# Splitting four weight blocks by one cast and one subtraction in a decoder layer with two feed-forward halves

## The chip, the cores and the metric

One core of a Trainium2 chip runs the whole layer as one program. The metric is the device time of one execution in microseconds (us), of which the median of three runs is quoted. The engines are named as in the profile: PE (matmul) with PEld (its weight loads), DVE (vector engine), ACT (scalar engine), POOL, and SP, whose queue issues all the transfers spoken of here.

## The reference

The reference is one decoder layer on 256 tokens of 2048 values in float32: a first SwiGLU half step, a mixing part (differential attention and a convolution group between one input and one output projection), cross-attention into 256 memory tokens, and a second SwiGLU half step. The change touches the two half steps (called FFN1 and FFN2 here):

```python
def swiglu(h, w_gate, w_up, w_down):
    return (jax.nn.silu(h @ w_gate) * (h @ w_up)) @ w_down

x = x + 0.5 * swiglu(rms_norm(x, ffn1_norm_g[l]), ffn1_w_gate[l], ffn1_w_up[l], ffn1_w_down[l])
...
x = x + 0.5 * swiglu(rms_norm(x, ffn2_norm_g[l]), ffn2_w_gate[l], ffn2_w_up[l], ffn2_w_down[l])
```

The weights are 2048x5632 (gate, up) and 5632x2048 (down), in float32.

## The kernel before

**Split numbers.** A float32 product is made of three matmuls on a rounded format (fp32r): every operand is split into a high part (a cast) and a low part (the operand minus the high part), and high x high, high x low and low x high are added in PSUM. The activations are split once. Every weight block must be split when it arrives: `split` (line 145) issues a cast on ACT (line 146) that writes a tile `wh`, and a subtraction on DVE (line 147) that reads the landed weights `raw` and `wh` and writes `wl`. A block is 128 rows by 512 columns.

**Parts.** `quad` (line 200) does the FFN products. It works through parts; a part is two 128-row blocks of each of two weight matrices, so four blocks, in one tile `raw` of 128x4x512. Two transfers on SP's queue bring them (lines 228 and 229; one 512 KB each). There are three `raw` tiles (`RAWS` = 3, line 27). For an ordinary part the four blocks are split by two casts and two subtractions of 1024 columns (lines 230 and 234), and PE does 24 matmuls of 512 columns (lines 278 to 282). A part with sums, called a seven here, multiplies a 2x2 arrangement of blocks by seven products instead of eight: three of the blocks are split as they come (two by one cast and one subtraction of 1024 columns, line 230, the third by one of 512, line 232), DVE makes sums of the blocks in place in `raw` (lines 242, 244 and 245: 1024, 512 and 512 columns), and the four results are split by two more casts and subtractions of 1024 columns (lines 247 and 248). PE then does 21 matmuls (`passes`, line 195, called in lines 260 to 266). The split tiles come in pairs `wh`, `wl` of two blocks each from the pool `wf`, which holds seven of each (`SPLITS`, lines 27, 141 and 411); an ordinary part takes two pairs, a seven takes four.

**Chunks and passes.** `ffn` (line 410) goes through 11 chunks of 512 gate and up columns, in groups of 4, 4 and 3. A chunk is one call of `quad` with 8 parts, of which parts 1, 3 and 5 are sevens (`S_IN`, line 29); only the very first chunk of FFN1 has none. After a group two passes of the down product follow, each with 8 parts and three sevens, or, for the group of 3, with 6 parts and two sevens (`S_DOWN`, `ORDER_DOWN`, lines 33 and 34). In both half steps together there are 264 parts, of which 95 are sevens, 168 ordinary, and one, the first of all, is split block by block (lines 217 to 226).

**What ends a chunk.** After the last seven `middle` (line 429) calls `combine` (line 287): ACT copies the PSUM tile `p1`, DVE forms `us` from the PSUM tile `q6` (line 292), then `vw` (line 294) and `ys` (line 432). At the end of the chunk `evac` (line 436) adds these to the PSUM sums into new tiles `full` (line 441), takes the silu into a new tile `s` on ACT (line 444) and multiplies on DVE (line 446). `turn` (line 449), due seven steps later, or two after the last chunk of a group, transposes the result on PE (line 452). The transposed blocks go to PSUM tiles of the same two slots (`tpp`) that `p1` and `q6` occupied, so the second group of transposes can start only when `us` has been computed.

**Order.** The program states the order of the work; the tool that builds the program places instructions of each engine in an order of its own by its estimate of when they can run, and each engine then runs its queue in that fixed order. `later` and `step` (lines 71 to 83) say after how many parts deferred work is stated.

**Between the half steps.** Pools opened after FFN1 (lines 644 to 647: `memp`, the weight pools of the middle part, and `mix` in line 688) take the memory that FFN1's pools had, and FFN2's pools take theirs. `proj` (line 150), which does all the products in between, splits two blocks at a time by one cast and one subtraction.

Of the kernel before, what the change touches and what calls it, by code (L numbers as in the profile page):

```python
# [7 lines left out]
F32 = mybir.dt.float32  # L8
F32R = mybir.dt.float32r
# [3 lines left out]
ALU = mybir.AluOpType  # L13
# [3 lines left out]
P = 128  # L17
# [6 lines left out]
START_S = 6  # L24
LOADS_X = (1, 2, 2, 3, 3, 4, 4, 4)
WARM = 8
RAWS, SPLITS, H_BUFS = 3, 7, 2

S_IN = (1, 3, 5)
ORDER_0 = tuple(range(8))  # L30
# [23 lines left out]
def hybrid_layer(ctx, tc, x, head, xT, mem, memT, pos, convw, bvec, w):  # L54
    nc = tc.nc
    V, S, T, G = nc.vector, nc.scalar, nc.tensor, nc.gpsimd
# [9 lines left out]
    ph = {}  # L66
# [60 lines left out]
    def behind(ins):  # L127

        order = ExitStack()
        for i in ins:  # L130
            order.enter_context(tc.issue_after(i.ins))
        return order
# [3 lines left out]
            fn()  # L136

    def weight_tiles():
        return ph["raw"].tile([P, 2, 512], F32, tag="raw", name="raw"), *split_tiles()

    def split_tiles():
        return (ph["wh"].tile([P, 2, 512], F32R, tag="wh", name="wh"),
                ph["wl"].tile([P, 2, 512], F32R, tag="wl", name="wl"))

    def split(raw, wh, wl):
        last[:] = [S.copy(out=wh, in_=raw),  # L146
                   V.tensor_tensor(out=wl, in0=raw, in1=wh.bitcast(F32), op=ALU.subtract)]  # L147
# [44 lines left out]
    def rows_pair(wsrc, row):  # L192
        return wsrc[row * P:(row + 2) * P, :].rearrange("(c p) n -> p c n", p=P)
# [6 lines left out]
    def quad(parts, srcs, middle, evac, first=False):  # L200

        acc = [[accp.tile([P, 512], F32, tag=f"acc{tb}{j}", name=f"acc{tb}{j}") for j in range(2)]
               for tb in range(2)]
        begun = set()
        seven = [i for i, p in enumerate(parts) if p()[4]]  # L210
        q = None
        for n, part in enumerate(parts):
            h, l, i0, row, sums = part()

            raw = ph["raw"].tile([P, 4, 512], F32, tag="raw", name="raw")
            wa, wb = split_tiles(), split_tiles()
            if first and n == 0:

                for b in range(2):
                    for j in range(2):  # L220
                        pos = (0, 1, 3, 2)[2 * b + j]
                        nc.sync.dma_start(out=raw[:, pos, :], in_=srcs[j][(row + b) * P:(row + b + 1) * P, :])
                        t = wa if pos < 2 else wb
                        with behind(first_x):
                            split(raw[:, pos, :], t[0][:, pos % 2, :], t[1][:, pos % 2, :])
                    first_hooks[b]()
            else:
                nc.sync.dma_start(out=raw[:, 0:4:3, :], in_=rows_pair(srcs[0], row))
                nc.sync.dma_start(out=raw[:, 1:3, :], in_=rows_pair(srcs[1], row))
                split(raw[:, 0:2, :], *wa)  # L230
                if sums:
                    split(raw[:, 3, :], wb[0][:, 1, :], wb[1][:, 1, :])
                else:
                    split(raw[:, 2:4, :], *wb)
            ev0, ev1, od1, od0 = [tuple(t[:, c, :] for t in w) for w in (wa, wb) for c in range(2)]

            def at(b, tb):
                return [t[:, i0 + b, tb * P:(tb + 1) * P] for t in (h, l)]

            if sums:  # L240

                V.tensor_tensor(out=raw[:, 1:3, :], in0=raw[:, 1:3, :], in1=raw[:, 2:4, :], op=ALU.add)  # L242

                V.tensor_tensor(out=raw[:, 3, :], in0=raw[:, 3, :], in1=raw[:, 1, :], op=ALU.add)
                V.tensor_tensor(out=raw[:, 0, :], in0=raw[:, 0, :], in1=raw[:, 3, :], op=ALU.add)
                wc, wd = split_tiles(), split_tiles()
                split(raw[:, 1:3, :], *wc)
                split(raw[:, 0:4:3, :], *wd)
                t3, t1, t4, t2 = [tuple(t[:, c, :] for t in w) for w in (wc, wd) for c in range(2)]
                sh, sl = sums  # L250

                def s(c):
                    return [t[:, c, :] for t in (sh, sl)]

                if q is None:
                    q = {"p1": tpp.tile([P, 512], F32, tag="tp", name="p1"),
                         "q6": tpp.tile([P, 512], F32, tag="tp", name="q6"),
                         "q57": ph["q"].tile([P, 2, 512], F32, tag="q57", name="q57")}
                st, sp = n == seven[0], n == seven[-1]
                passes(acc[0][0], *at(0, 0), ev0, "00" not in begun, False)  # L260
                passes(acc[0][1], *s(3), ev1, "01" not in begun, False)
                passes(q["p1"], *at(1, 0), od0, st, sp)
                passes(q["q57"][:, 1, :], *s(2), t3, st, sp)
                passes(q["q57"][:, 0, :], *s(0), t1, st, sp)
                passes(acc[1][0], *at(0, 1), t4, "10" not in begun, False)
                passes(q["q6"], *s(1), t2, st, sp)
                begun |= {"00", "01", "10"}
                if sp:
                    middle(q)
            else:  # L270
                ending = n == len(parts) - 1
                wt = [[ev0, ev1], [od0, od1]]
                for tb in range(2):
                    for js in ([[0], [1]] if ending else [[0, 1]]):
                        for b in range(2):
                            hs, ls = at(b, tb)
                            for j in js:
                                T.matmul(acc[tb][j], hs, wt[b][j][0], start=f"{tb}{j}" not in begun, stop=False)  # L278
                                begun.add(f"{tb}{j}")
                                T.matmul(acc[tb][j], hs, wt[b][j][1], start=False, stop=False)  # L280
                            for j in js:
                                T.matmul(acc[tb][j], ls, wt[b][j][0], start=False, stop=(ending and b == 1))  # L282
                    if ending:
                        evac(tb, acc[tb])
            step()
# [122 lines left out]


    def ffn(norm, wg, wu, wd, groups, done):  # L410
        with tc.tile_pool(name="wf", bufs=SPLITS, reuse_waits="tile") as wf, \
                tc.tile_pool(name="ffn", bufs=2, reuse_waits="tile") as fp, \
                tc.tile_pool(name="ht", bufs=max(groups), reuse_waits="tile") as hp, \
                tc.tile_pool(name="wfr", bufs=RAWS, reuse_waits="tile") as wfr, \
                tc.tile_pool(name="qp", bufs=1, space=PSUM) as qp:
            ph.update(h=hp, raw=wfr, wh=wf, wl=wf, f=fp, q=qp, sraw="sraw", xsf="xsf")
            c0 = 0
            for gi, ng in enumerate(groups):
                hts, hsums, hold = {}, {}, {}
                s_down = S_DOWN[ng]  # L420
                for c in range(c0, c0 + ng):
# [5 lines left out]
                    rest = {}  # L427
# [8 lines left out]
                    def evac(tb, acc, c=c, rest=rest, end=(c == c0 + ng - 1), pairs=(c - c0 < s_down)):  # L436
                        acc = list(acc)
                        for j in range(2):
                            if rest:
                                t = fp.tile([P, 512], F32, tag="full", name="full")  # L440
                                V.tensor_tensor(out=t, in0=acc[j], in1=rest[tb, j][0], op=rest[tb, j][1])
                                acc[j] = t
                        s = fp.tile([P, 512], F32, tag="s", name="s")
                        S.activation(out=s, in_=acc[0], func=AF.Silu, scale=norm.rs(tb))
                        h = fp.tile([P, 512], F32, tag="h", name="h", bufs=H_BUFS)
                        V.scalar_tensor_tensor(out=h, in0=acc[1], scalar=norm.rs(tb), in1=s,
# [125 lines left out]
        V.tensor_scalar(out=xqcol, in0=col(C_XQ), scalar1=P ** -0.5, scalar2=None, op0=ALU.mult)  # L572

    def constants_b():
        bv = ph["f"].tile([P, 384], F32, name="bv", bufs=1)
        nc.sync.dma_start(out=bv, in_=bvec.broadcast_to([P, 384]))
        lm = stat.tile([P, 2, 64], F32, tag="cs", name="lm", bufs=1)
        b4 = bv[:, :256].rearrange("p (a b d) -> p a b d", a=2, b=2)
# [45 lines left out]
        for qk in range(2):  # L624
            g = bv[:, 256 + 64 * qk:256 + 64 * qk + 16]
            for tb in range(2):
                for hf in range(2):
# [3 lines left out]
                                    op=ALU.mult)  # L631
                    V.scalar_tensor_tensor(out=ropeB[:, tb, qk, hf * 8:(hf + 1) * 8], in0=sn[:, tb, :],
                                           scalar=(1.0 if hf else -1.0), in1=go, op0=ALU.mult, op1=ALU.mult)

    later(10, lambda: behind_last(constants_a))
    later(11, lambda: behind_last(constants_b))

    n2 = Norm(G_MIX, "mix")
# [3 lines left out]

    mids = ctx.enter_context(ExitStack())
    memp = mids.enter_context(tc.tile_pool(name="memp", bufs=1, reuse_waits="tile"))
    for kind, bufs in (("wh", 5), ("raw", 4), ("wl", 5)):
        ph[kind] = mids.enter_context(tc.tile_pool(name="m" + kind, bufs=bufs, reuse_waits="tile"))
    atp = mids.enter_context(tc.tile_pool(name="atp", bufs=2, space=PSUM))
# [25 lines left out]
    for n in range(4):  # L673
        later(6 + 6 * n, lambda n=n: mem_group(n))

    kmT = memp.tile([P, 4, 256], F32, name="kmT")
    vm = [memp.tile([P, 512], F32, name=f"vm{tb}") for tb in range(2)]

    def mstats():
        return [(mgrp[k // 4][0], mgrp[k // 4][1], k % 4, k) for k in range(KD)]  # L680
# [7 lines left out]
    with tc.tile_pool(name="mix", bufs=1, reuse_waits="tile") as mp:  # L688
        uT = [mp.tile([P, 4, 30 + 256], F32, name=f"uT{c}") for c in range(2)]
        y = mp.tile([P, 8, 256], F32, name="y")  # L690
        vt = [[mp.tile([P, 512], F32, name=f"v{tb}{c}") for c in range(2)] for tb in range(2)]
        for c in range(2):
            G.memset(uT[c][:, :, 0:30], 0.0)

# [212 lines left out]
        for ct in range(8):  # L907
# [4 lines left out]
            for j in range(1, TAPS):  # L912
                V.scalar_tensor_tensor(out=yc, in0=u[:, j:j + 256], scalar=cw[:, j * 8 + ct:j * 8 + ct + 1],  # L913
                                       in1=yc, op0=ALU.mult, op1=ALU.add)
# [7 lines left out]
        for a in range(2):  # L922
            V.tensor_tensor(out=y[:, 4 * a:4 * a + 4, :], in0=y[:, 4 * a:4 * a + 4, :],
                            in1=pm.broadcast_to([P, 4, 256]), op=ALU.subtract)
# [136 lines left out]
    out = w["out"]  # L1061
# [45 lines left out]
```

## Time and profile before

| what | value |
|---|---|
| median of three runs | 1887.45 us (1886.5 to 1888.75) |
| the profiled execution's own time | 1892.69 us |
| its span in the profile | 1890.9 us |
| busy: PE, PEld, DVE, ACT | 1857.8, 1526.2, 1682.3, 1091.6 us |
| granted TensorE clock, mean | 0.996 of full speed |
| read from HBM | 361.09 MB, 192 GB/s over the span |

The span is the stretch from the first to the last instruction of the profiled execution; its own time is 1.8 us longer and is 5.24 us above the median of the runs shown. Busy time of PE counts the modelled length of matmuls that overlap, so how close PE is to its pace is read from the distance between the starts of matmuls and from its gaps.

### The profile page before, as it was taken

Reading aid. Unit: us, or ns where it says so; the run is one execution under the profiler, and the core shown is the slowest. Engines: PE = TensorE matmul, PEld = TensorE weight load, DVE = VectorE, ACT = ScalarE, POOL = GpSimd, SP = SyncE. Lnnn points to the kernel's source line nnn. Section 1 sums busy time; section 2 is a strip of 40 time slices with the busy share of each in tenths; the row PEclk is TensorE's granted clock in tenths of the full one; section 3 lists DMA queues with packets and bytes.
Section 4 is the critical chain, followed back from the end, with each engine's and each line's share of the span. In section 5 each row is a group of like instructions: output and inputs, shape, how many; then the busy total and the mean of one; then the engine's idle time right before and its main releaser. Section 6 shows DMA issues by size and latency. Waiting matters only on the chain.

```text
span 1890.9 us, 23351 instructions
## 1 busy us (share of the span) xinstructions
PE 1857.8 (98%) x8365; PEld 1526.2 (81%) x8365; DVE 1682.3 (89%) x2246; ACT 1091.6 (58%) x1462; POOL 24.8 (1%) x29
## 2 busy tenths in 40 slices
PE   8999999999999999999999999999999999999998
PEld 6887888888888787888777887888788888888887
DVE  7898999999999996699998656999899999899998
ACT  7655455565555555454577656665555655545653
POOL 0000000000000000000011000000000000000000
PEclk9999999999999999999999999999999999999999
DMA  9555556656665655666543751556565665646554
GB/s 332 188 200 198 181 166 219 212 184 199 204 220 178 200 167 180 221 212 211 178 135 110 257 186 60 200 181 219 181 198 201 221 207 196 195 160 223 192 188 155
DMA packets 188756, 364.72 MB, mean 193 GB/s; under 512 B 11616, under 2 KB 12128, under 8 KB 188640
## 3 DMA queue, kind: packets, MB, share of 16 engines
q1 hardware_dynamic: 188640, 363.23, 58.2%
q8 instruction: 65, 1.06, 0.2%
q14 instruction: 51, 0.42, 0.1%
HBM read 361.09 MB, written 2.10 MB: 192 GB/s over the span
## 4 chain that ended last, share of the span: by engine, by line
PE 66%; DVE 22%; DMA 5%; ACT 4%; issue 2%; POOL 1%; SPq 0%; ACTq 0%; DVEq 0%
PE acc L282 13%; PE acc L280 13%; PE acc L278 13%; DVE wl L147 9%; DVE y L913 4%; PE acc L185 3%; PE acc L183 3%; PE acc L182 3%; ACT wh L146 3%; DMA raw<-ffn_w_up 3%; PE acc L198 2%; PE acc L197 2%; PE acc L196 2%; PE q L198 2%; PE q L196 2%
## 5 line engine op out<-in xcount | busy, mean ns | idle before, releaser
L146 ACT CAST wh<-raw 128x1024 fp32r<-128x1024 f32 (+1 forms) x864 | 842.3, 1002 | 651.4 <-DVE raw L242 252.4
L147 DVE TENSOR_TENSOR wl<-raw,wh 128x1024 fp32r<-128x1024 f32 (+1 forms) x864 | 977.6, 1160 | 154.2 <-ACT wh L146 139.1
L278 PE MATMUL acc<-wh,xh_f 128*128 128x512 f32 x904 | 354.8, 395 | 6.0 <-ACT wh L146 5.2
L280 PE MATMUL acc<-wl,xh_f 128*128 128x512 f32 x904 | 354.3, 393 | 0.6 <-DVE wl L147 0.5
L282 PE MATMUL acc<-wh,xl_f 128*128 128x512 f32 x904 | 295.6, 391 | 0.0
L278 PEld LDWEIGHTS acc<-wh,xh_f 128*128 128x128 f32 x904 | 170.7, 189 | 44.4 <-ACT wh L146 8.0
L280 PEld LDWEIGHTS acc<-wl,xh_f 128*128 128x128 f32 x904 | 171.1, 190 | 36.0 <-DVE wl L147 1.7
L282 PEld LDWEIGHTS acc<-wh,xl_f 128*128 128x128 f32 x904 | 170.8, 189 | 35.5
L278 PE MATMUL acc<-wh,hth 128*128 128x512 f32 x448 | 174.5, 391 | 0.3 <-DVE x L481 0.3
L280 PE MATMUL acc<-wl,hth 128*128 128x512 f32 x448 | 174.5, 390 | 0.0
L282 PE MATMUL acc<-wh,htl 128*128 128x512 f32 x448 | 147.9, 390 | 0.0
L182 PE MATMUL acc<-wh,xh_mix 128*128 128x512 f32 x320 | 125.8, 394 | 1.8 <-ACT wh L146 1.8
L183 PE MATMUL acc<-wl,xh_mix 128*128 128x512 f32 x320 | 125.3, 392 | 0.5 <-DVE wl L147 0.5
L242 DVE TENSOR_TENSOR raw<-raw 128x1024 f32<-128x1024 f32 x95 | 115.7, 1218 | 0.0
L198 PE MATMUL q<-wh,sl 128*128 128x512 f32 x285 | 110.9, 389 | 0.0
L197 PE MATMUL q<-wl,sh 128*128 128x512 f32 x285 | 110.9, 389 | 0.0
L196 PE MATMUL q<-wh,sh 128*128 128x512 f32 x285 | 110.9, 389 | 0.0
L185 PE MATMUL acc<-wh,xl_mix 128*128 128x512 f32 x320 | 102.8, 391 | 0.0
L913 DVE SCALAR_TENSOR_TENSOR y<-uT,cw,y 128x256 f32<-128x256 f32 x240 | 102.6, 484 | 0.1
L278 PEld LDWEIGHTS acc<-wh,hth 128*128 128x128 f32 x448 | 84.1, 188 | 18.2 <-DVE x L481 0.7
L282 PEld LDWEIGHTS acc<-wh,htl 128*128 128x128 f32 x448 | 84.1, 188 | 17.6
L280 PEld LDWEIGHTS acc<-wl,hth 128*128 128x128 f32 x448 | 84.2, 188 | 17.1
(297 smaller groups left out, 2518.5 us busy)
## 6 DMA issues: line engine op xcount, KB each, us to landing
raw<-ffn_w_down SPq DMA_DIRECT2D x176, 512.0 KB, 4.9
raw<-ffn_w_gate SPq DMA_DIRECT2D x175, 512.0 KB, 4.1
raw<-ffn_w_up SPq DMA_DIRECT2D x175, 512.0 KB, 5.2
raw<-w_in SPq DMA_DIRECT2D x80, 512.0 KB, 4.5
raw<-w_out SPq DMA_DIRECT2D x32, 512.0 KB, 4.7
raw<-xattn_w_kv SPq DMA_DIRECT2D x16, 512.0 KB, 4.0
raw<-xattn_w_q SPq DMA_DIRECT2D x8, 512.0 KB, 4.0
raw<-xattn_w_o SPq DMA_DIRECT2D x8, 512.0 KB, 3.8
```

Of the source, the lines that this page charges most:

```text
L146: last[:] = [S.copy(out=wh, in_=raw), V.tensor_tensor(out=wl, in0=raw, in1=wh.bitcast(F32), op=ALU.subtract)]
L147: V.tensor_tensor(out=wl, in0=raw, in1=wh.bitcast(F32), op=ALU.subtract)]
L182: T.matmul(acc[tb][j], hs, wt[k, j][0], start=(fresh and k == 0), stop=False)
L183: T.matmul(acc[tb][j], hs, wt[k, j][1], start=False, stop=False)
L185: T.matmul(acc[tb][j], ls, wt[k, j][0], start=False, stop=(ending and k == nk - 1))
L196: T.matmul(acc, hs, w[0], start=start, stop=False)
L197: T.matmul(acc, hs, w[1], start=False, stop=False)
L198: T.matmul(acc, ls, w[0], start=False, stop=stop)
L278: T.matmul(acc[tb][j], hs, wt[b][j][0], start=f"{tb}{j}" not in begun, stop=False)
L280: T.matmul(acc[tb][j], hs, wt[b][j][1], start=False, stop=False)
L282: T.matmul(acc[tb][j], ls, wt[b][j][0], start=False, stop=(ending and b == 1))
L913: V.scalar_tensor_tensor(out=yc, in0=u[:, j:j + 256], scalar=cw[:, j * 8 + ct:j * 8 + ct + 1], in1=yc, op0=ALU.mult, op1=ALU.add)
```

## The change

Only the two half steps are touched, and the places of some tiles. In `quad` an ordinary part is split by one cast and one subtraction of four blocks (2048 columns). A seven is split by one of three blocks (1536 columns) and, after the sums, one of four; the sums are the same three additions at other places of `raw`. The split tiles hold four blocks; there are four places, each with a `wh` and a `wl`, taken in turn, one by an ordinary part and two by a seven. `evac` adds into the tile of `rest`, and the silu overwrites its input. The tile `xsf` shares the place of `ys`. A tile `bv` of 640 columns is laid out first in each half step's pool. `kmT`, `vm` and the first half of `vt` move to a pool `kvp` of their own, opened before the weight pools of the middle part.

```diff
-RAWS, SPLITS, H_BUFS = 3, 7, 2
+RAWS, SPLITS, H_BUFS = 3, 4, 2
...
     def split_tiles():
-        return (ph["wh"].tile([P, 2, 512], F32R, tag="wh", name="wh"),
-                ph["wl"].tile([P, 2, 512], F32R, tag="wl", name="wl"))
+
+        i = places[0] % SPLITS
+        places[0] += 1
+        return tuple(ph["w4"].tile([P, 4, 512], F32R, tag=f"{t}{i}", name=f"{t}{i}") for t in ("wh", "wl"))
...
-            wa, wb = split_tiles(), split_tiles()
+            wa = split_tiles()
...
-                nc.sync.dma_start(out=raw[:, 0:4:3, :], in_=rows_pair(srcs[0], row))
-                nc.sync.dma_start(out=raw[:, 1:3, :], in_=rows_pair(srcs[1], row))
-                split(raw[:, 0:2, :], *wa)
+                for j in range(2):
+                    nc.sync.dma_start(out=raw[:, j:4:2, :], in_=rows_pair(srcs[j], row))
                 if sums:
-                    split(raw[:, 3, :], wb[0][:, 1, :], wb[1][:, 1, :])
+                    split(raw[:, 0:3, :], *[t[:, 0:3, :] for t in wa])
                 else:
-                    split(raw[:, 2:4, :], *wb)
+                    split(raw, *wa)
...
-                V.tensor_tensor(out=raw[:, 1:3, :], in0=raw[:, 1:3, :], in1=raw[:, 2:4, :], op=ALU.add)
-
-                V.tensor_tensor(out=raw[:, 3, :], in0=raw[:, 3, :], in1=raw[:, 1, :], op=ALU.add)
-                V.tensor_tensor(out=raw[:, 0, :], in0=raw[:, 0, :], in1=raw[:, 3, :], op=ALU.add)
-                wc, wd = split_tiles(), split_tiles()
-                split(raw[:, 1:3, :], *wc)
-                split(raw[:, 0:4:3, :], *wd)
+                V.tensor_tensor(out=raw[:, 1:4:2, :], in0=raw[:, 1:4:2, :], in1=raw[:, 3:1:-1, :], op=ALU.add)
+
+                V.tensor_tensor(out=raw[:, 2, :], in0=raw[:, 2, :], in1=raw[:, 1, :], op=ALU.add)
+                V.tensor_tensor(out=raw[:, 0, :], in0=raw[:, 0, :], in1=raw[:, 2, :], op=ALU.add)
+                wb = split_tiles()
+                split(raw, *wb)
...
-            ph.update(h=hp, raw=wfr, wh=wf, wl=wf, f=fp, q=qp, sraw="sraw", xsf="xsf")
+            ph.update(h=hp, raw=wfr, w4=wf, f=fp, q=qp, sraw="sraw", xsf="y")
+            fp.tile([P, 640], F32, tag="bv", name="bv", bufs=1)
...
-                                t = fp.tile([P, 512], F32, tag="full", name="full")
-                                V.tensor_tensor(out=t, in0=acc[j], in1=rest[tb, j][0], op=rest[tb, j][1])
+                                t = rest[tb, j][0]
+                                V.tensor_tensor(out=t, in0=acc[j], in1=t, op=rest[tb, j][1])
...
-                        s = fp.tile([P, 512], F32, tag="s", name="s")
+                        s = acc[0] if rest else fp.tile([P, 512], F32, tag="p1", name="s", bufs=1)
...
+    kvp = mids.enter_context(tc.tile_pool(name="kvp", bufs=1, reuse_waits="tile"))
...
-    kmT = memp.tile([P, 4, 256], F32, name="kmT")
-    vm = [memp.tile([P, 512], F32, name=f"vm{tb}") for tb in range(2)]
+    kmT = kvp.tile([P, 4, 256], F32, name="kmT")
+    vm = [kvp.tile([P, 512], F32, name=f"vm{tb}") for tb in range(2)]
...
-        vt = [[mp.tile([P, 512], F32, name=f"v{tb}{c}") for c in range(2)] for tb in range(2)]
+        vt = [[(kvp, mp)[tb].tile([P, 512], F32, name=f"v{tb}{c}") for c in range(2)] for tb in range(2)]
```

## Rows read from the trace of the kernel before

**Rows 1.** The page's first part: busy time, share, instructions of each engine.

```profile
PE 1857.8 (98%) x8365; PEld 1526.2 (81%) x8365; DVE 1682.3 (89%) x2246; ACT 1091.6 (58%) x1462; POOL 24.8 (1%) x29
```

**Rows 2.** By stretch: us, busy PE, PEld, DVE, ACT, POOL (instructions), clock, DMA; chunk, down pass.

```profile
1513.60:1556.42 42.82, 42.63 (x191) 35.04 (x192) 40.12 (x48) 25.76 (x30) 0.00 (x0) 1.00 0.59 195
...
1388.00:1429.50 41.50, 41.50 (x185) 34.34 (x184) 38.88 (x42) 21.94 (x24) 0.00 (x0) 1.00 0.63 201
```

**Rows 3.** Waits: engine, line, releaser: us in total, times, longest.

```profile
PE tp L452 <- DVE us L292: 8.8, 11, 2.3
...
SPq L228 <- DVE wl L147: 1036.1, 240, 16.0
```

**Rows 4.** Timeline before the second transposes of a chunk (start, us, what).

```profile
1597.54 1.23 DVE L147 TENSOR_TENSOR wl<-raw,wh 128x1024 fp32r<-128x1024 f32 x1 [0.63 <-ACT wh L146]
...
1598.68 0.68 DVE L292 TENSOR_TENSOR us<-q,p1s 128x512 f32<-128x512 f32 x1
...
1599.42 0.66 PE L452 MATMUL tp<-ident,h 128*128 128x128 f32 x4 [0.38 <-DVE us L292]
```

**Rows 5.** Groups by form: busy us, mean ns | idle before, releasers.

```profile
L147 DVE TENSOR_TENSOR wl<-raw,wh 128x1024 fp32r<-128x1024 f32 x765 | 915.6, 1222 | 150.7 <-ACT wh L146 135.8
...
L147 DVE TENSOR_TENSOR wl<-raw,wh 128x512 fp32r<-128x512 f32 x99 | 67.8, 684 | 3.5 <-ACT wh L146 3.3
...
L146 ACT CAST wh<-raw 128x1024 fp32r<-128x1024 f32 x765 | 783.9, 1051 | 610.5 <-DVE raw L242 252.4 <-PE acc L185 125.6 <-PE acc L282 104.6
L146 ACT CAST wh<-raw 128x512 fp32r<-128x512 f32 x99 | 61.4, 620 | 40.9 <-PE acc L282 21.2 <-PE acc L198 12.9 <-DVE x L476 5.4
```

**Rows 6.** Timeline, DVE: a subtraction and the instruction right behind it.

```profile
1513.46 1.22 DVE L147 TENSOR_TENSOR wl<-raw,wh 128x1024 fp32r<-128x1024 f32 x1
...
1514.59 1.22 DVE L294 TENSOR_TENSOR vw<-q,us 128x1024 f32<-128x1024 f32 x1
```

**Rows 7.** Timeline, DVE and ACT: the sums of a seven inside a chunk of FFN1.

```profile
111.03 1.22 DVE L242 TENSOR_TENSOR raw<-raw 128x1024 f32<-128x1024 f32 x1
...
113.01 0.69 DVE L245 TENSOR_TENSOR raw<-raw 128x512 f32<-128x512 f32 x1
113.62 1.22 DVE L147 TENSOR_TENSOR wl<-raw,wh 128x1024 fp32r<-128x1024 f32 x1
113.81 1.05 ACT L146 CAST wh<-raw 128x1024 fp32r<-128x1024 f32 x1 [0.40 <-DVE raw L245]
```

**Rows 8.** Timeline, DVE: first and last of nine instructions behind line 242 in another seven.

```profile
1521.27 0.68 DVE L307 TENSOR_TENSOR sl<-sraw,sh 128x512 fp32r<-128x512 f32 x1
...
1526.13 0.74 DVE L446 SCALAR_TENSOR_TENSOR h<-full,rstd_f,s 128x512 f32<-128x512 f32 x1
```

**Rows 9.** Timeline at the second part of FFN1: ACT and PE.

```profile
14.57 2.00 ACT L146 CAST wh<-raw 128x1024 fp32r<-128x1024 f32 x2 [1.87 <-DMA raw<-ffn_w_up]
...
15.67 0.73 PE L278 MATMUL acc<-wh,xh_f 128*128 128x512 f32 x2 [4.13 <-ACT wh L146]
```

**Rows 10.** The chain of waits at the first part of FFN2 (start, us, what).

```profile
1179.70 1.05 ACT wh L146
...
1182.05 0.73 PE acc L280 x2
```

**Rows 11.** The chain of waits at the end of FFN2's first group.

```profile
1334.77 5.76 DMA raw<-ffn_w_down
...
1340.63 1.05 ACT wh L146
...
1341.71 1.23 DVE wl L147
...
1343.59 0.66 PE tp L452 x4
```

**Rows 12.** By stretch, columns as in rows 2: right after that gap.

```profile
1343.00:1345.50 2.50, 1.91 (x9) 1.63 (x10) 2.50 (x3) 1.64 (x3) 0.00 (x0) 0.83 0.94 359
1345.50:1348.00 2.50, 2.50 (x7) 1.91 (x7) 2.50 (x5) 0.37 (x1) 0.00 (x0) 0.50 0.83 228
```

More of the change, by code (lines that the diff above doesn't have):

```diff
@@ L138, in weight_tiles @@
     def weight_tiles():
-        return ph["raw"].tile([P, 2, 512], F32, tag="raw", name="raw"), *split_tiles()
+        return (ph["raw"].tile([P, 2, 512], F32, tag="raw", name="raw"),
+                ph["wh"].tile([P, 2, 512], F32R, tag="wh", name="wh"),
+                ph["wl"].tile([P, 2, 512], F32R, tag="wl", name="wl"))
+    places = [0]
     def split_tiles():
-        return (ph["wh"].tile([P, 2, 512], F32R, tag="wh", name="wh"),
-                ph["wl"].tile([P, 2, 512], F32R, tag="wl", name="wl"))
+        i = places[0] % SPLITS
+        places[0] += 1
+        return tuple(ph["w4"].tile([P, 4, 512], F32R, tag=f"{t}{i}", name=f"{t}{i}") for t in ("wh", "wl"))
     def split(raw, wh, wl):
@@ L220, in quad @@
                     for j in range(2):
-                        pos = (0, 1, 3, 2)[2 * b + j]
+                        pos = 2 * b + j
                         nc.sync.dma_start(out=raw[:, pos, :], in_=srcs[j][(row + b) * P:(row + b + 1) * P, :])
-                        t = wa if pos < 2 else wb
                         with behind(first_x):
-                            split(raw[:, pos, :], t[0][:, pos % 2, :], t[1][:, pos % 2, :])
+                            split(raw[:, pos, :], *[t[:, pos, :] for t in wa])
                     first_hooks[b]()
             else:
-                nc.sync.dma_start(out=raw[:, 0:4:3, :], in_=rows_pair(srcs[0], row))
-                nc.sync.dma_start(out=raw[:, 1:3, :], in_=rows_pair(srcs[1], row))
-                split(raw[:, 0:2, :], *wa)
+                for j in range(2):
+                    nc.sync.dma_start(out=raw[:, j:4:2, :], in_=rows_pair(srcs[j], row))
                 if sums:
-                    split(raw[:, 3, :], wb[0][:, 1, :], wb[1][:, 1, :])
+                    split(raw[:, 0:3, :], *[t[:, 0:3, :] for t in wa])
                 else:
-                    split(raw[:, 2:4, :], *wb)
-            ev0, ev1, od1, od0 = [tuple(t[:, c, :] for t in w) for w in (wa, wb) for c in range(2)]
+                    split(raw, *wa)
+            ev0, ev1, od0, od1 = [tuple(t[:, c, :] for t in wa) for c in range(4)]
             def at(b, tb):
@@ L240, in quad @@
             if sums:
-                V.tensor_tensor(out=raw[:, 1:3, :], in0=raw[:, 1:3, :], in1=raw[:, 2:4, :], op=ALU.add)
-                V.tensor_tensor(out=raw[:, 3, :], in0=raw[:, 3, :], in1=raw[:, 1, :], op=ALU.add)
-                V.tensor_tensor(out=raw[:, 0, :], in0=raw[:, 0, :], in1=raw[:, 3, :], op=ALU.add)
-                wc, wd = split_tiles(), split_tiles()
-                split(raw[:, 1:3, :], *wc)
-                split(raw[:, 0:4:3, :], *wd)
-                t3, t1, t4, t2 = [tuple(t[:, c, :] for t in w) for w in (wc, wd) for c in range(2)]
+                V.tensor_tensor(out=raw[:, 1:4:2, :], in0=raw[:, 1:4:2, :], in1=raw[:, 3:1:-1, :], op=ALU.add)
[3 more added lines that the diff above has]
+                split(raw, *wb)
+                t4, t3, t2, t1 = [tuple(t[:, c, :] for t in wb) for c in range(4)]
                 sh, sl = sums
@@ L410, in ffn @@
     def ffn(norm, wg, wu, wd, groups, done):
-        with tc.tile_pool(name="wf", bufs=SPLITS, reuse_waits="tile") as wf, \
+        with tc.tile_pool(name="wf", bufs=1, reuse_waits="tile") as wf, \
                 tc.tile_pool(name="ffn", bufs=2, reuse_waits="tile") as fp, \
@@ L574, in constants_b @@
     def constants_b():
-        bv = ph["f"].tile([P, 384], F32, name="bv", bufs=1)
+        bv = ph["f"].tile([P, 640], F32, tag="bv", name="bv", bufs=1)[:, :384]
         nc.sync.dma_start(out=bv, in_=bvec.broadcast_to([P, 384]))
```

## The prediction

> **What bounds the kernel now.** I read the busy shares first: PE 98%, DVE 89%, ACT 58% [rows 1]. The share of PE alone doesn't say how much is left, so I went to the busy time by stretch. In a chunk of FFN2 PE is busy for 42.63 of 42.82 us, and in a pass of the down product for all of 41.50 [rows 2]; a chunk has 3 x 21 + 5 x 24 = 183 matmuls of 512 columns, as has the pass, so one takes 0.227 us. The change leaves their number as it is, so in these stretches it can win only the gaps. DVE is next: 40.12 of 42.82 us in the chunk and 38.88 of 41.50 in the pass, which leaves it a room of 2.7 and 2.6 us. The waits then say where PE stops inside the half steps: 11 times, 8.8 us together, before the second transposes of a chunk, for `us` on DVE [rows 3]. The timeline shows how: a subtraction of a weight split stands in DVE's queue just ahead of `us`, so `us` starts when it ends, and PE waits 0.38 us [rows 4]. [...]
>
> **Fewer instructions.** By the two sizes, 512 more columns cost 1222 - 684 = 538 ns on DVE and 1051 - 620 = 431 ns on ACT [rows 5]. So 2048 columns take an estimated 684 + 3 x 538 = 2298 ns on DVE and 620 + 3 x 431 = 1913 ns on ACT; 1536 take 1760 and 1482. A seven goes from four splits to two, an ordinary part from two to one: 95 x 2 + 168 = 358 subtractions and casts fewer. What one is worth to DVE I take from neighbours in its queue: behind a subtraction of 1.22 us the next instruction starts after 1.13 us [rows 6], 1024 columns at the slope above are 1.08 us, so some 0.07 us of an instruction's fixed cost is not hidden by its neighbour (by the slope alone 0.05). 358 x 0.07 = 25 us less work for DVE, 11 x 0.07 = 0.8 us in a chunk (three sevens, five ordinary parts). ACT saves more, but it is 58% busy. None of this lies on PE's path; it widens DVE's room in a chunk to 2.7 + 0.8 = 3.5 us. [...]
>
> **A new wait in every seven.** Now the first subtraction behind the sums starts at 113.62, 0.61 us after the last sum (line 245) started: its cast had to wait for line 242 only and was done [rows 7]. With one cast of all four blocks the cast must wait for the last sum. ACT starts 0.80 us after that sum's start (113.81), takes 1.91, and with 0.03 us to hand over the subtraction starts 2.74 us after, so 2.13 us later than now. In that time DVE waits, unless its queue has other work there. 95 sevens make 202 us of waits; a chunk has 3 x 2.13 = 6.4 us against a room of 3.5. The queue does get filled from elsewhere: in the first seven of a chunk nine other instructions of the chunk's end stand between line 242 and the splits [rows 8], so I take that wait as covered, and in a down pass one by the additions to x. Two are left, 4.26 us, or 0.76 us over the room. The next part's subtraction can cover more where its weights have landed and its place is free; between nothing more and all of it I take half, 0.38 us, in the 21 chunks that have sevens and the 8 long down passes: 29 x 0.38 = 11 us. The 4 short passes (two sevens, one covered) stay inside their room: 0. The ends are 0 (covered, or DVE's saving goes to it) and 29 x (6.4 - 3.5) + 4 x 1.7 = 91 us.
>
> **The first parts.** Where PE already waits for a split, the longer cast is on its path. At FFN1's second part the first of two casts of 1.05 us ends the wait of PE [rows 9]; one cast of 1.91 ends it 0.86 us later, and its low part 0.86 + 1.08 = 1.94 us later. FFN2's first part is the same: cast, subtraction, matmul from 1179.70 to 1182.05 [rows 10]. Each costs 0 to 1.9 us; FFN1's is partly hidden, since the weights behind it are late too. I take 1 us each: +2.
>
> **The transposes.** The 11 waits for `us` [rows 3] can go either way. A subtraction of 2.3 us ahead of `us` holds it 1.08 us longer: 11 x 1.08 = +12 us at most. But it also becomes ready 0.86 us later, behind the longer cast, and then `us` may stand ahead of it: -8.8 us at most. The row is near the middle (`us` starts 1.14 us after the subtraction did [rows 4]), so 0. [...]
>
> **The rest** I cost at nothing. Transfers keep their number and sizes. The places hold 16 blocks instead of 14; an ordinary part's place comes free two parts before it is needed, about 4.8 + 5.4 us of matmuls against 4.2 us of cast and subtraction. The in-place additions and silu have the same instructions; the next writer of `p1` and `vw` comes five parts later. Moved pools change what the first tiles of a new pool must wait for; nothing in the trace prices it, from -2 to +2 us around the two changes of pools.
>
> **Sum.** 0 + 11 + 2 + 0 = +13 us, on the profiled execution's own time: 1892.7 + 13 = 1905.7. That execution is 5.2 us above the median shown, so 1900.5, say 1900 us. A measurement of this kernel can tell 0.2% (3.8 us) from no change.
>
> **Rivals.** (1) *Shorter DVE work closes the gaps.* If the queue is filled in most sevens and `us` moves ahead of the long subtraction, PE loses the 8.8 us [rows 3] and the clock of the two long gaps, 2 x 1.7 [rows 12]: up to -12, less 2 for the first parts, so -4 to -12, 1875 to 1883 us. For it: the order is made anew and rows 8 show such filling. Against it: DVE's room is no cause of those gaps, the order is. (2) *DVE, or the weights' tiles, becomes the bound.* A `raw` tile is freed only by its last subtraction, for which the queue waits already [rows 3]; in a seven that comes 2 us later, and the next transfer, 5.8 us [rows 11], with it. With three tiles, a pair of a seven and an ordinary part then needs up to 10.8 us (1.7 + 2.6 for three blocks and sums, 2.1 of wait, 2 x 2.2) where PE needs 45 matmuls, 10.2 us. If none of the waits is covered it costs 91 us; it decides once less than 2.9 of the 6.4 us a chunk are covered. At half to full price 1930 to 1978 us. (3) *Nothing shows.* The waits fit the room, first parts and transposes cancel: 1884 to 1891 us. [...]
>
> **Chances.** Forecast 0.40 (own range 1889 to 1915; 0.36 of it slower, 0.04 within 0.2%), rival 1 0.32 (0.30 faster, 0.02 within), rival 2 0.14 (slower), rival 3 0.14 (0.04 faster, 0.10 within). Faster 0.34, same 0.16, slower 0.50. The range runs from the far end of rival 1 to the cheap end of rival 2 and leaves out most of rival 2, some 0.12: 1874 to 1938 us.
>
> **What would show it.** Right: in sevens of the new trace the subtraction waits about 2 us for its cast in one or two of three, DVE's busy share per chunk near 94% with idle time put down to the cast, and PE gaps under 1 us spread over the chunks. Rival 1: the transposes' wait is gone from the list and chunks last 42.6 us. Rival 2: chunks of 44 us and more, PE waiting at lines 278 and 280 for casts and subtractions. The forecast is wrong if the subtraction of 2048 columns takes much more or less than 2.3 us, or if the queue is filled in all sevens.

## The result, and the profile after

The changed kernel takes **1904.75 us** (median of 4 runs, 1901.9 to 1908.0) against 1888.1 us for the kernel before in the same job (4 runs, 1886.5 to 1889.2): ratio 1.0089, 95% interval [1.0077, 1.0101]. It is 16.7 us slower; the forecast, 1900 us, lay 12.6 us above the median it started from (1887.45). The profiled execution has a span of 1906.2 us, 15.3 more than before, and a time of 1908.0.

The page's first part of the kernel after:

```profile
PE 1873.2 (98%) x8365; PEld 1521.7 (80%) x8365; DVE 1656.1 (87%) x1888; ACT 1036.4 (54%) x1104; POOL 24.2 (1%) x29
```

Against [rows 1] DVE has 358 instructions fewer and 26.2 us less work, ACT 55 us less. PE does the same 8365 matmuls, its share is 98% again, and its *busy time* has grown by 15.4 us, as much as the span. So the loss does not show as idle time of PE (33.0 us of the span, before 33.1): matmul ends are modelled, and many of the new stops are so short that they disappear in the time drawn for a matmul, 0.39 us where the starts lie 0.227 us apart. PE's weight loads show them better. The waits of the kernel after (engine, line, releaser: us in total, times, longest):

```profile
PEld q L203 <- DVE wl L153: 10.4, 33, 1.8
PEld q L202 <- ACT wh L152: 9.8, 21, 1.3
PEld tp L456 <- ACT p1s L293: 7.5, 9, 1.5
PEld tp L456 <- DVE us L295: 4.8, 15, 0.6
...
PE tp L456 <- ACT p1s L293: 3.7, 7, 1.1
...
DVE wl L153 <- ACT wh L152: 194.0, 179, 4.0
ACT wh L152 <- DMA raw<-ffn_w_up: 142.9, 68, 5.2
...
ACT wh L152 <- DVE raw L249: 88.4, 32, 4.9
...
SPq L234 <- DVE wl L153: 948.4, 240, 11.9
```

The first two lines are new: 54 waits, 20.2 us together, all at matmuls into `q`, which are the sevens' first users of the second split (t3, t1, t2). In the trace before no wait of this kind is among the weight loads' waits of 1 us or more. The loads for transposes waited 15.8 us there (16 times, for `us`) and wait 12.3 now, for `p1s` more than for `us`; PE's own wait of [rows 3] is down from 8.8 to 3.9 us. A weight load waits in part beside a matmul that is still drawn as running (before the matmul at 1250.33 us below the load had waited 1.77 us and PE 1.33), so these sums are upper bounds on lost time.

One seven in the timeline of the kernel after (start, us, what):

```profile
1244.19 1.22 DVE L246 TENSOR_TENSOR raw<-raw 128x1024 f32<-128x1024 f32 x1
...
1245.93 0.68 DVE L248 TENSOR_TENSOR raw<-raw 128x512 f32<-128x512 f32 x1
1246.04 3.71 ACT L152 CAST wh<-raw 128x2048 fp32r<-128x2048 f32 x2 [4.33 <-DVE raw L249]
...
1246.64 0.69 DVE L249 TENSOR_TENSOR raw<-raw 128x512 f32<-128x512 f32 x1
...
1247.99 4.49 DVE L153 TENSOR_TENSOR wl<-raw,wh 128x2048 fp32r<-128x2048 f32 x2 [0.65 <-ACT wh L152]
...
1248.60 0.40 PE L202 MATMUL q<-wh,sh 128*128 128x512 f32 x1
...
1250.33 0.49 PE L203 MATMUL q<-wl,sh 128*128 128x512 f32 x1 [1.33 <-DVE wl L153]
```

Two casts and two subtractions stand here back to back, the splits of two sevens. Each cast waits for a last sum (L249); ACT had idled 4.33 us before the first. PE had the high part for its first pass at 1248.60, where the next matmul would have followed after 0.23 us; the low part was through at 1250.3, and 1.5 us went. Before, the low parts of t3 and t1 came from a subtraction of 1.22 us whose cast did not wait for the last sum [rows 7].

The sizes, by form (busy us, mean ns | idle before, releasers), against [rows 5]:

```profile
L153 DVE TENSOR_TENSOR wl<-raw,wh 128x2048 fp32r<-128x2048 f32 x263 | 595.3, 2287 | 110.6 <-ACT wh L152 110.3
L152 ACT CAST wh<-raw 128x2048 fp32r<-128x2048 f32 x263 | 497.2, 1912 | 441.2 <-DMA raw<-ffn_w_up 110.2 <-PE acc L285 109.3 <-DVE raw L249 88.4
...
L153 DVE TENSOR_TENSOR wl<-raw,wh 128x1536 fp32r<-128x1536 f32 x95 | 166.5, 1752 | 16.1 <-ACT wh L152 16.0
```

By stretch (columns as in rows 2), the chunk and the pass that answer to those there, then FFN2's start:

```profile
1525.76:1568.58 42.82, 42.80 (x192) 34.39 (x190) 39.59 (x38) 23.65 (x20) 0.00 (x0) 1.00 0.59 202
1397.50:1439.00 41.50, 41.50 (x184) 34.00 (x183) 37.23 (x31) 20.16 (x12) 0.00 (x0) 1.00 0.60 203
1180.00:1190.00 10.00, 7.37 (x34) 5.45 (x32) 7.83 (x14) 8.41 (x17) 0.00 (x0) 0.90 0.00 1
1190.00:1195.50 5.50, 5.50 (x14) 4.34 (x15) 5.50 (x9) 3.56 (x6) 1.55 (x1) 0.55 0.83 250
1195.50:1200.00 4.50, 4.50 (x21) 3.73 (x20) 3.44 (x7) 2.43 (x2) 0.52 (x1) 1.00 0.42 161
```

This chunk and this pass are no slower than before, with less work on DVE. The loss is in other places: stops of 0.3 to 2 us scattered over the chunks, and FFN2's start, which the next lines of the timeline show:

```profile
1185.59 1.89 ACT L152 CAST wh<-raw 128x2048 fp32r<-128x2048 f32 x1
...
1187.52 2.29 DVE L153 TENSOR_TENSOR wl<-raw,wh 128x2048 fp32r<-128x2048 f32 x1 [1.11 <-ACT wh L152]
1187.54 1.61 PE L281 MATMUL acc<-wh,xh_f 128*128 128x512 f32 x4 [1.92 <-ACT wh L152]
...
1189.87 1.22 PE L283 MATMUL acc<-wl,xh_f 128*128 128x512 f32 x2 [0.72 <-DVE wl L153]
```

From cast to the first matmul on a low part 4.28 us pass (before 2.35 [rows 10]). PE idles 1.92 us, the granted clock falls (0.62 of full over the 2.5 us from 1187.5, in which PE idles 0.72 us more), and then it is 0.55 of full over 5.5 us, another 2.5 us; in the 3 us from 1191 it is 0.50, and matmuls of 512 columns start 0.43 us apart there, against 0.227 in the steady stretches.

A second way to find the loss is to subtract, for every n, the start of the n-th matmul before from that after. The difference grows by 2.1 us over the first 60 matmuls (FFN1's start) and from 5.9 to 10.1 us over the first 30 of FFN2: 6.3 us at the two starts. At three group ends it *shrinks*, by 3.9, 2.0 and 3.7 us. PE stopped there before, for `us`, 2.26, 1.91 and 2.29 us (at 175.9, 645.1 and 1343.6 us; 6.5 of the 8.8 us of [rows 3]), and behind the first and the last of these stops the clock fell to 0.50; after has none of the three. The end is at 15.3 us, so all the rest, the sevens among it, lost some 18.6 us in this pair of executions.

### The profile page after: what moved, and what is told of

The parts are those of the page before. It is cut to its first block, busy times and chain, and to the rows that moved or that the text cites. A ratio compares the mean times of both kernels' runs of the same rounds, so it can differ in the third digit from the quotient of the medians.

```text
span 1906.2 us, 22159 instructions
## 1 busy us (share of the span) xinstructions
PE 1873.2 (98%) x8365; PEld 1521.7 (80%) x8365; DVE 1656.1 (87%) x1888; ACT 1036.4 (54%) x1104; POOL 24.2 (1%) x29
## 4 chain that ended last, share of the span: by engine, by line
PE 55%; DVE 23%; DMA 9%; ACT 6%; issue 4%; SPq 1%; POOL 1%; DVEq 0%; ACTq 0%
DVE wl L153 12%; PE acc L283 10%; PE acc L285 10%; PE acc L281 10%; DMA raw<-ffn_w_up 7%; ACT wh L152 6%; PE acc L191 4%; PE acc L189 4%; PE acc L188 4%; DVE y L919 3%; PE q L203 2%; PE q L204 2%; PE q L202 2%; PE acc L204 2%; PE acc L203 2%
## 5 line engine op out<-in xcount | busy, mean ns | idle before, releaser
L152 ACT CAST wh<-raw 128x2048 fp32r<-128x2048 f32 (+3 forms) x506 | 787.3, 1576 | 711.8 <-PE acc L285 153.5
L153 DVE TENSOR_TENSOR wl<-raw,wh 128x2048 fp32r<-128x2048 f32 (+3 forms) x506 | 934.9, 1870 | 195.1 <-ACT wh L152 194.0
L285 PE MATMUL acc<-wh,xl_f 128*128 128x512 f32 x904 | 305.3, 393 | 0.0
L285 PEld LDWEIGHTS acc<-wh,htl 128*128 128x128 f32 x448 | 84.0, 188 | 17.4
```

The lines of the kernel that those rows point to most:

```text
L152: last[:] = [S.copy(out=wh, in_=raw), V.tensor_tensor(out=wl, in0=raw, in1=wh.bitcast(F32), op=ALU.subtract)]
```

## The experiments

The scheduler orders every engine's queue anew for each build, so each edit below also moves instructions that it doesn't name; a difference of 2 us between two of these kernels means little. All intervals are ratios to the kernel before on the same chip, whose median was 1888.3 to 1888.9 us.

### e1 to e4: which split

Diffs against the kernel after. e1, the seven's second split:

```
-                split(raw, *wb)
+                split(raw[:, 1:4:2, :], *[t[:, 1:4:2, :] for t in wb])
+                split(raw[:, 0:3:2, :], *[t[:, 0:3:2, :] for t in wb])
```

e2, the ordinary parts (e3 is e1 and e2 together):

```
-                    split(raw, *wa)
+                    split(raw[:, 0:2, :], *[t[:, 0:2, :] for t in wa])
+                    split(raw[:, 2:4, :], *[t[:, 2:4, :] for t in wa])
```

e4 is e3 with the seven's first split in two as well:

```
-                    split(raw[:, 0:3, :], *[t[:, 0:3, :] for t in wa])
+                    split(raw[:, 0:2, :], *[t[:, 0:2, :] for t in wa])
+                    split(raw[:, 2, :], *[t[:, 2, :] for t in wa])
```

> The kernel after, with the second split of each seven done again as two casts and two subtractions of 1024 columns (t3 and t1 first, then t4 and t2), so that the first two final blocks are split without waiting for the last sum. Theory (the new wait in every seven): the weight loads' waits of the sevens' first matmuls on these blocks, 20.2 us after (10.4 on the subtraction in 33 places, 9.8 on the cast in 21), fall below 5 us, and the time falls by 8 to 15 us, to 1890 to 1897. Rival (the ordinary parts' longer first cast and subtraction cost the time): the time stays within 3 us of after, 1902 to 1908.

Measured: 1892.46 us, 1.0024 [1.0015, 1.0032]: 12.3 us below after, as the theory had it. A wait of e1's weight loads:

```profile
PEld acc L203 <- DVE wl L153: 9.0, 19, 1.4
```

The waits for `q` are gone but for 0.9 us. This line is a new one: matmuls into `acc`, which wait for a subtraction elsewhere. e9 below takes it up.

> The kernel after, with the split of each ordinary part done again as two casts and two subtractions of 1024 columns; sevens as after. Theory (the wait is in the sevens): only the start of FFN2, where after stands 4.5 us further behind than at its end of the mixing part, and some of FFN1's start come back: 2 to 6 us, 1899 to 1903. Rival (the ordinary parts cost the time): 10 us or more come back, 1895 or less.

Measured: 1902.36 us, 1.0066 [1.0051, 1.0080], 2.4 us below after (4.3 by the ratios). The rival falls.

> Both: only the first split of a seven stays in one piece (1536 columns), all others are of 1024. Theory: the gains of both add up, 1884 to 1892, as fast as before or somewhat faster, since the long transposes' waits at the group ends (8.8 us before) stay gone. Rival (what costs is something else in the change, the tiles of four in turn or the in-place additions): it stays above 1897.

Measured: 1887.31 us, 0.9995 [0.9985, 1.0005]: 17.4 us below after, and no different from before. The two splits explain the whole loss. Whether they simply add up is open: halving the ordinary parts gives 2.4 us (4.3 by the ratios) where the sevens are long and 5.2 (5.5) where they are halved, and the intervals leave some 3 us either way.

> All splits as before (2 of 1024 in an ordinary part; 1024, 512 and twice 1024 in a seven); tiles of four in turn, in-place silu and additions and the pools as after. Theory: this part of the change costs nothing, 1884 to 1891. Rival (tiles of four come free later, since a whole tile waits for its last reader): slower than before by 4 us or more, 1892 to 1900.

Measured: 1889.77 us, 1.0004 [0.9995, 1.0013]. The tiles in turn, the in-place operations and the pools together are worth nothing that can be measured. A surprise lies in the traces: the gap at the first group's end of FFN2 [rows 11, 12], and its like, are gone in the profiled execution of e4 too, and its median is still that of before.

### e5: the wait without the length

Diff against e3:

```
-                split(raw[:, 1:4:2, :], *[t[:, 1:4:2, :] for t in wb])
-                split(raw[:, 0:3:2, :], *[t[:, 0:3:2, :] for t in wb])
+                split(raw[:, 0:2, :], *[t[:, 0:2, :] for t in wb])
+                split(raw[:, 2:4, :], *[t[:, 2:4, :] for t in wb])
```

> The kernel e3 (1887.3: the seven's second split in two of 1024, t3 and t1 first) with the two halves paired otherwise: blocks 0 and 1 (t4, t3) first, 2 and 3 (t2, t1) second. The sizes and the number of instructions are those of e3, but the first cast has to wait for the seven's last sum, as in after. Theory (the wait for the last sum is what costs): the weight loads' waits on wh and wl in the sevens come back by 8 us or more, and the time rises by 6 to 11 us, to 1893 to 1898. Rival (the length of a cast and a subtraction of 2048, which come 2.1 us later to an end, is what costs, whatever they wait for): within 3 us of e3, 1885 to 1890.

Measured: 1896.34 us, 1.0038 [1.0023, 1.0052], 9.0 us above e3 (8.1 by the ratios, since e3 ran in another job). With equal sizes and numbers the other pairing costs 9.0 us; from here to e2 (splits of 2048 in the sevens), the length costs another 6.0 (5.3). So both theories have a part. The pairing changes two things, though: the first cast waits for the last sum, and t1, which was in the first half, comes with the second. The runs don't part these two. The place was only half right, as the waits of e5 show:

```profile
PEld q L203 <- DVE wl L153: 3.8, 10, 0.9
PEld q L202 <- ACT wh L152: 1.9, 9, 0.3
PEld acc L203 <- DVE wl L153: 1.1, 1, 1.1
```

These are 6.8 us, 5.9 more than in e3, not 8. In this execution another part is lost at a group's end: counted by the n-th matmul, 5.4 of the 10.4 us by which the traces of e3 and e5 differ come within 50 matmuls there. The timeline of e5 there:

```profile
1647.48 2.00 ACT L152 CAST wh<-raw 128x1024 fp32r<-128x1024 f32 x2 [5.27 <-DMA raw<-ffn_w_down]
...
1648.56 1.23 DVE L153 TENSOR_TENSOR wl<-raw,wh 128x1024 fp32r<-128x1024 f32 x1 [3.53 <-ACT wh L152]
...
1649.70 1.22 DVE L299 TENSOR_TENSOR vw<-q,us 128x1024 f32<-128x1024 f32 x1
...
1650.84 0.68 DVE L487 SCALAR_TENSOR_TENSOR x<-acc,x 128x512 f32<-128x512 f32 x1
...
1651.66 0.47 PE L283 MATMUL acc<-wh,hth 128*128 128x512 f32 x1 [1.92 <-DVE x L487]
```

It is the chain of [rows 11] with another end: a subtraction that waits for a cast that waits for a load, and behind it in DVE's queue the addition that PE needs. Which execution and which build has it can't be told from single traces, so how much of the 9.0 us lies in the sevens is open.

### e6 and e10: the first parts

e6 is e1 with the ordinary parts of each FFN's first chunk in halves; e10 has the same edit on the kernel after.

```
-                    split(raw, *wa)
+                    for lo in ((0, 2) if halves else (0,)):
+                        hi = lo + 2 if halves else 4
+                        split(raw[:, lo:hi, :], *[t[:, lo:hi, :] for t in wa])
...
-middle, evac, first=start)
+middle, evac, first=start, halves=c == 0)
```

> The kernel e1 (1892.5: sevens in halves, ordinary parts in one piece) with the ordinary parts of the first chunk of each FFN in halves as well (5 and 8 parts of 95). Between e1 and e3 (all ordinary parts in halves) lie 5.2 us. Theory (only where the loads have just begun does the larger first cast come late): nearly all of it comes back, 1887 to 1890. Rival (it is spread over all ordinary parts): within 1.5 us of e1, 1891 to 1894.

Measured: 1886.15 us, 0.9986 [0.9975, 0.9996], 6.3 us below e1, a little more than the theory had. (The expectation miscounts the parts: DVE has 12 instructions more than in e1, for 12 of 168 ordinary parts.) These 12 are worth all that e3 had over e1, and the other 156 may be merged. In the profiled executions, compared at equal numbers of matmuls, e6 is ahead of e1 by 2.4 us behind FFN1's start, of which 0.9 are left some 400 matmuls later; it gains 1.5 in the mixing part, which the edit doesn't touch, and 1.9 at FFN2's start, and ends 5.5 ahead. So the two starts show, but not all of the difference lies there.

> The kernel after with nothing undone but the ordinary parts of the first chunk of each FFN (12 parts), which are split in halves again. Theory (two terms that add up): what this gave in the sevens' absence, 6.3 us from e1 to e6, comes here too: 1896 to 1901. Rival (the sevens' waits behind the start take it up again, since all 168 ordinary parts in halves gave only 2.4 us): 1901 to 1906.

Measured: 1904.56 us, 1.0087 [1.0073, 1.0101], 0.2 us below after: the rival holds, within intervals that leave some 3 us either way. The profiled executions differ by 3.6 us, and FFN2's start is mended in e10 (by stretch, columns as in rows 2; compare the clock of 0.55 after):

```profile
1176.00:1186.00 10.00, 8.88 (x43) 6.85 (x41) 8.58 (x18) 8.30 (x19) 1.38 (x1) 1.00 0.00 1
1186.00:1192.00 6.00, 6.00 (x28) 4.97 (x28) 6.00 (x11) 4.88 (x8) 0.33 (x1) 1.00 0.76 213
```

The medians don't show it. The two traces show where it goes: e10 is 3.7 us ahead of after before FFN2's start and 7.9 ahead behind it, but over the next 250 matmuls this falls to 4.5, by stops of 0.7, 0.7 and 1.2 us that after doesn't have (two before ordinary parts, one in a seven), and at the end it is 3.8. A start that comes earlier is held up again behind it; with the sevens' second splits halved (e6) it counts. One pair of executions shows the loss; that the sevens are its reason is argued from the medians, not shown.

### e7, e8 and e11: the raw tiles and the rest

```
-RAWS, SPLITS, H_BUFS = 3, 4, 2
+RAWS, SPLITS, H_BUFS = 4, 3, 2
```

> The kernel after with four raw tiles in place of three, and three pairs of split tiles in place of four (both four don't fit). Rival (a raw tile, now held until a cast and a subtraction of all four blocks are through, is what makes the loads late: casts waited 142.9 us for loads of ffn_w_up after, 33.1 before): faster than after by 4 us or more, 1901 or less. Theory (the sevens wait for their own last sum, not for loads): the same or slower, 1903 to 1912, the slower the more the fourth pair of split tiles was worth.

Measured: 1970.25 us, 1.0424 [1.0404, 1.0444]. Much slower than either side had it: nothing is learned of the raw tiles, but a good deal of the split tiles. Its waits:

```profile
PEld acc L281 <- ACT wh L152: 65.1, 81, 4.9
```

With three pairs in turn the cast of an ordinary part comes too late 81 times. Three are too few.

e11 is the kernel before with the in-place operations and the pools of after; e8 is e11 with `RAWS` 4 in place of 3.

> The kernel before (tiles of two blocks, all splits as before) with the in-place additions and the pools of after, and the room that these leave spent on a fourth raw tile. Theory (three raw tiles are enough there): 1886 to 1891, as before. Rival (loads wait for raw tiles in steady chunks): faster than before by 4 us or more, 1884 or less.

> The kernel before with the in-place silu and additions and the pools of after alone (three raw tiles, tiles of two blocks). Theory (they cost and give nothing): 1886 to 1891, within 0.2% of before, and e8 (1886.5 with a fourth raw tile) within 3 us of it. Rival (the in-place additions hold the accumulators or p1s longer, and the next chunk's combine waits): 1892 or more.

Measured: e8 1886.47 us, 0.9987 [0.9976, 0.9998]; e11 1890.23, 1.0010 [1.0001, 1.0019]. The in-place part costs 1.3 us, barely out of its uncertainty, and the fourth raw tile gives 3.8 (4.3 by the ratios), a little over the 3 that e11's expectation allowed. So three raw tiles seem not quite enough even with the short splits. Neither kernel is a clean part of after, though: in both traces PE stops at FFN2's start (in e11 for 2.47 us before transposes, line 330, and for 2.38 before its first matmul, with a clock of 0.57 over the 12 us from 1178), and neither before nor after stops at those transposes. Whether a fourth would help the kernel after wasn't tried: e7, which has one, gave up a pair of split tiles for it.

### e9: a faster version

Against e6, the seven's first split as in e4's diff (1024 and 512).

> The kernel e6 (1886.2: sevens' second split in halves, the first chunk's ordinary parts in halves) with the first split of each seven as 1024 and 512 again in place of 1536. In e6 weight loads of a seven's first matmuls wait 8.0 us in 20 places for the subtraction of that first split. Theory (any split that spans blocks needed at different times costs what its first block waits): these waits go, and the time falls by 2 to 7 us, to 1879 to 1884. Rival (95 instruction pairs more take up what the waits gave: e3 with 1536 was 2.5 us below e4 with 1024 and 512): 1886 to 1890.

Measured: 1882.68 us, 0.9973 [0.9965, 0.9982], faster than both kernels and 22 us below after. Its waits:

```profile
PEld acc L203 <- DVE wl L153: 3.0, 6, 0.9
PEld q L203 <- DVE wl L153: 2.7, 9, 0.7
```

e6 had 8.0 us on the first (20 times) and 0.4 on the second, so this split's wait is mostly gone and a little of the next has come. Between e3 and e4 the same edit went the other way by 2.5 us, so its own size is open; the sum is not. In e9 156 of 168 ordinary parts are split in one piece, and every block of a seven that is needed early has a split that ends early.

## Why the prediction was right

**Direction and size.** +12.6 us on the median were forecast, +16.7 measured. The wait that the forecast named is the right one: the halves of the sevens' second split alone take back 12.3 us (e1), 15.1 where the ordinary parts are halved too (e2 to e3), and the waits for it are new lines of the trace. That the sum came so near is in part luck. In the two profiled executions its terms were 18.6 us for the sevens with all else, 6.3 for the first parts and -9.6 for the group ends, where it had 11, 2 and 0.

**Fewer instructions: right in the durations, lucky in the total.** The durations are 2287 and 1752 ns against 2298 and 1760 on DVE, 1912 and 1483 against 1913 and 1482 on ACT. 358 instructions fewer came with 26.2 us less work on DVE against 25. But e4, with as many DVE instructions as before (2246), has 10.7 of these 26.2 us already (1671.6 against 1682.3), so 15.5, 0.04 each, came with the merging itself; why e4 has less isn't known. The step's rows give 0.05 by the slope, or 18 us; no row and no run shows its 0.07. DVE's room gave nothing back to PE, as costed. Not every nanosecond that doesn't grow with the columns is saved: by the two sizes of [rows 5] these are 684 - 538 = 146 ns on DVE, which would be an estimated 358 x 0.146 = 52 us, and no more than 26.2 were measured, so the distance between neighbours in the queue was the better row.

**A new wait in every seven: right in size, the way to it only in part.** The step set DVE's waits against DVE's room. DVE's waits for casts grew from 139.1 to 194.0 us, by 55 and not by 202 us. The sign that was asked for, about 2 us in one or two sevens of three, did not come: directly behind the last sum the long subtraction waits 1.8 to 2.1 us in 17 of the 95 sevens, and 0.5 to 1.4 in 41 more. So the queue was filled in part or whole in most sevens, and DVE still has room (39.59 of 42.82 us, 92% and not the 94% expected). What PE lost in the sevens, it lost because the blocks that it needs first come later (20.2 us of waits of the weight loads, 12.3 us of the time back in e1), whether DVE had other work meanwhile or not. By e5 9.0 us go with the pairing (the wait for the last sum, the later t1, and in one execution a group's end) and 6.0 with the mere length. Nor did [rows 8] show a covered wait: two of the nine instructions are sums of the seven itself, and only one, of 0.74 us, stands behind the last sum, where the wait begins. The step had the length in its 2.13 us, but priced the whole at what DVE could not cover. That half of 0.76 us in 29 places came to 11 is luck: a size that fits, by a way that the trace does not show.

**The first parts: mis-sized.** +2 us were taken. The split is late as described (1.9 us from cast to low part), but the step left out the clock behind a longer gap, 2.5 us at FFN2's start, and the two starts cost 6.3 us in the trace. Undone alone the term is worth 0.2 us (e10), undone where the sevens are mended 6.3 (e6). It is a term that depends on the one behind it, and a sum of independent terms can't hold that.

**The transposes: it went the way of the gain.** The row was taken as undecided. PE's wait went from 8.8 to 3.9 us, and the long gaps at the group ends ([rows 11, 12]; three, two of them with a slow clock) have no counterpart after, which in this pair of traces is worth 9.6 us. A subtraction of a split stands directly ahead of `us` in 20 of 33 places, 30 before, as the lower bound supposed. How much of it is worth anything in the median is open: e4 has lost these gaps too and is as fast as before. Of the kernel before there is one trace, and its execution lies 4.6 us above the median of the four runs, about what one such gap with its clock costs: 2.29 us and, by [rows 12], (0.17 + 0.50) x 2.5 = 1.7 us, the 1.7 of rival 1. The 12 us that a longer subtraction ahead of `us` could have cost did not come; it was in the sevens that shorter splits let PE go on sooner (12.3 us, e1).

**The rest: right.** e4 and e11 are within 0.2% of before, e11 with a stop of its own at FFN2's start.

**Rivals.** Rival 1's first sign came in part (the transposes' waits shrank but are not gone), its second didn't (chunks of 42.6 us). Rival 2 did not come: the steady chunk still takes 42.8 us. SP's waits for a subtraction to free a raw tile are shorter (948.4 us against 1036.1), but 70.6 and 35.5 us of its waits are now put down to earlier transfers of ffn_w_up and ffn_w_down (before 1.3 and 0.9), so in all SP waits about as long; and casts wait more for loads (142.9 against 33.1 us for ffn_w_up). That these later loads cost little follows from e6, which keeps 156 long ordinary splits and is as fast as before. Rival 3 is excluded by the interval.

## What to carry to other kernels

Before several blocks are put through one instruction, ask for each block when its consumer wants it and when its input is ready: in the seven shown above the merged cast started only behind the last sum, ACT having idled 4.33 us, the subtraction behind it took some 2.3 us, and PE, which was waiting for one block's low part, lost 1.5 us. Merge where all blocks are wanted late (156 ordinary parts here, at no cost that can be measured), keep apart where one is wanted early (sevens, first parts); the 26.2 us of work saved on DVE, which had room, were worth nothing here. And where PE's busy share stays at 98% while the time grows, as here by 16.7 us, look at the waits of the weight loads: 20.2 us of new ones stood there, of which PE's idle time showed 3.0.

## What the runs showed that was not expected

- PE's busy time for the same 8365 matmuls differs by up to 41 us (1855.0 in e8, 1895.9 in e7), and by 15.4 between before and after, as much as the spans. It is no measure of work done.
- After an idle time of 1.92 us at FFN2's start the granted clock fell, and behind another of 0.72 it was 0.55 over the next 5.5 us; at the same place in e10, with 1.12 us idle in 10, it stayed at 1.00. Idle time 1.5 us longer cost 2.5 us more behind it. It is no rule: a stop of 1.91 us before (at 645.1 us) was followed by a clock of 1.00.
- One pair of split tiles in four is worth 65 us (e7, with a raw tile more), a fourth raw tile some 4 us (e8 against e11).
- Undoing one part of a change (the first parts) gave 0.2 or 6.3 us, according to what stood beside it.
- The same execution can win and lose: after won 9.6 us at three group ends and lost 24.9 elsewhere, and the sum alone shows neither.
